# Seven products for two steps in layer A's pairs of heads, and the scores' second transposition put ahead of them

## The chip, the cores and the metric

The kernel runs on one core of a Trainium2 chip. The metric is the device time of one execution in microseconds (us), the median of several runs; lower is better.

## The reference

Two layers over x of 256 rows and 2048 columns, fp32, 32 heads of 128. What matters here, cut down:

```python
# layer A
h = rms_norm(x, a_norm)
q, k, v, g = split(h @ a_w_in, 4)             # 2048 -> 4 x 4096
o = chunked attention(q, k, v, rel_bias)      # chunks of 64, bias by distance
x = x + (o * silu(g)) @ a_w_out               # 4096 -> 2048
# shared keys and values, forget gates
k, v = split(rms_norm(x, kv_norm) @ kv_w, 2); logf = log_sigmoid(h_kv @ f_w + f_b)
# layer B
q, g = split(rms_norm(x, b_norm) @ b_w_in, 2)
o = causal attention(q, k, v) with decay from cumsum(logf)
x = x + (o * silu(g)) @ b_w_out
return rms_norm(x, final_norm)
```

## The kernel before

**Products.** Every fp32 weight and activation is split into a high and a low part (fp32r), and a product is three matmuls: high x high, low x high, high x low. Activations lie on the partitions transposed (`xTh`, `xTl`: normalised x of layer A), 256 rows are two tiles of 128. A *unit* is 512 output columns. In layer A each pair of heads g (0 to 15) has two units, `aqk{g}` (q and k) and `avg{g}` (v and gate). Their inner dimension of 2048 is done in 8 *steps* of two blocks of 128 (`KB`); a step is 2 blocks x 2 row tiles x 3 = 12 matmuls of 128x512 into `acc[0]`, `acc[1]` (PSUM).

**Feed.** SyncE's queue loads each step's weights (512 KB) into one of six `raw` buffers. ScalarE writes the high part (L247), VectorE the low part (L248); both go to one of `SPLIT = 4` buffers, so that a step's split can begin only when TensorE is through with the step four places before. `get()` hands a step to TensorE and keeps the splits three ahead (`DEPTH`).

**Quads.** In the output projections (`ao`, `bo`) some steps of two units go as a *quad*: four blocks of a 2x2 product (two row tiles, two k blocks) for two units by seven products in place of eight, as Winograd's form of Strassen's scheme has it. Two raw buffers `one` and `two` (the same step of the first and second unit) give four items: `one`; the differences `t` (L287, L288); half of `two`; and differences written back into `one` (L296, L297). Each is split like a step (L293 high, L294 low, the third with half the size). The left sides are the blocks of the activations and their sums (`sums`, made by `open`). Seven products of three matmuls are 21 instead of 24. Three go straight into `acc`; the others (p1, p5, p7, p6) stay in PSUM and are put together in `comb` at the end, which is then added to the units' results.

**Order.** Each engine runs its instructions in the order in which they stand, written down by a scheduling layer from the program's order. The attention of pair g runs as a generator (`side_a`) during pair g+1; the tables `QK_STEPS`, `PV_STEPS`, `OLD_A_STEPS` say after which step how many of its parts are issued. Its parts: `turn` of q and k (a VectorE transposition of 32x32 blocks and 16 small DMAs, into `turned`), splits (`wideh`/`widel`, `q1h`/`q1l`, `q0`), scores (`s1p`, `s0p` on TensorE), softmax (`sg`: scale and bias, maximum, exponentials, reciprocal, and the gate scaled by it), a second `turn` (`sgY`, 16 DMAs to `sgZ`), its split, the product with v (`op`), gating. When a unit ends, ScalarE evacuates `qk` from PSUM (L495), and `close_vg` makes v (`vh`, `vl`, `v1`) and the gate (`gs`) from `avg`'s accumulators. `feed.behind` ties an instruction to a place in ScalarE's order by a tiny write that reads a split's high part.

**Projections.** `xin` is the residual input of an output unit; it is loaded with four steps left, in one buffer (tag `R`) that several tiles share. At the end of a unit of `ao`, VectorE adds `comb` (L751) and the accumulators (L753) to it; its rows are transposed into `x1T`, the last unit's by TensorE (`x_to_T`, L169) inside the first steps of layer B, where `bqg0` already runs.

Of the kernel before, what the change touches and what calls it, by code (L numbers as in the profile page):

```python
# [16 lines left out]
P = 128  # L17
# [38 lines left out]

QK_STEPS = {0: 1, 6: 1, 7: 2}
PV_STEPS = {1: 1}
OLD_A_STEPS = {0: 1, 2: 99}
B1_STEPS = {3: 1, 5: 1, 6: 2}  # L60
# [15 lines left out]
def trunk(ctx, tc, x, x_t, gains, a_w_in, a_rel, a_w_out, kv_w, f_w, f_b, b_w_in, b_w_out, final_norm, out):  # L76
# [200 lines left out]
    class Quad:  # L277
# [4 lines left out]
        def split(self, i):  # L282

            one, two = self.raw
            t = self.all.t[:, 0]
            if not i:
                dve.tensor_sub(t[:, :, 0], two[:, :, 0], one[:, :, 0])  # L287
                dve.tensor_sub(t[:, :, 1], two[:, :, 1], two[:, :, 0])  # L288
            src = [one, t, two[:, :, 1:], one][i]
            n = src.shape[2]  # L290
            hi = stream.tile([P, IL, KB, HN], F32R, name=f"quad_hi{i}", tag="hi", bufs=SPLIT)
            lo = stream.tile([P, IL, KB, HN], F32R, name=f"quad_lo{i}", tag="lo", bufs=SPLIT)
            act.activation(hi[:, :, :n], src, AF.Copy)  # L293
            dve.tensor_sub(lo[:, :, :n], src, r32(hi[:, :, :n]))  # L294
            if not i:
                dve.tensor_sub(one[:, :, 0], two[:, :, 1], t[:, :, 0])  # L296
                dve.tensor_sub(one[:, :, 1], one[:, :, 1], one[:, :, 0])  # L297
            return hi, lo

        def step(self, lhs, first, second):  # L300
# [33 lines left out]
            if self.last:  # L334
                c = q.comb = q.t.rearrange("p r a j n -> p (r a j n)").rearrange("p (i n) -> p i n", n=UN)
                act.activation(c[:, 0], p1, AF.Copy)
                dve.tensor_add(c[:, 3], c[:, 0], p6)
                dve.tensor_add(c[:, 2], c[:, 3], p5)
                dve.tensor_add(c[:, 1], c[:, 3], p7)
                dve.tensor_add(c[:, 3], c[:, 1], p5)  # L340

    class Quads:


        def __init__(self, name, w):
            self.name, self.w, self.sums = name, w, []

# [10 lines left out]
        def open(self, lhs, n):  # L358


            self.t = big_tile([P, 2, IL, KB, HN], F32, f"{self.name}_quad")
            free = self.t[:, 1].rearrange("p a j n -> p (a j n)").rearrange("p (c i s) -> p c i s", c=2, s=P)
            xs, v = free[:, 0].rearrange("p (k t) s -> p k (t s)", t=NT), free[:, 1]
            for b in range(n):
                if b % 2 == 0:
                    two = big_tile([P, 2, 2, 4, P], F32R, f"{self.name}_sums{b}")
                self.sums.append(two[:, b % 2])
                hi, lo = two[:, b % 2, 0], two[:, b % 2, 1]
                k = b * KB
                dve.tensor_add(xs, r32(lhs.hi[k // BIG][:, k % BIG:k % BIG + KB]),  # L370
                               r32(lhs.lo[k // BIG][:, k % BIG:k % BIG + KB]))
                a11, a21, a12, a22 = (xs[:, j, t * P:(t + 1) * P] for j in range(KB) for t in range(NT))
                dve.tensor_add(v[:, 0], a21, a22)
                dve.tensor_sub(v[:, 2], a11, a21)
                dve.tensor_sub(v[:, 1], v[:, 0], a11)
                dve.tensor_sub(v[:, 3], a12, v[:, 1])
                act.activation(hi, v, AF.Copy)
                dve.tensor_sub(lo, v, r32(hi))
                yield

    def spec(name, w, nk, late=0, kept=0, g0=None):


        return dict(name=name, w=w, nk=nk, late=late, kept=kept, g0=g0)

    def whole(spec):
        return [(spec, b) for b in range(spec["nk"] // KB)]

    qkvg = []
    for g in range(NG):  # L390
        qkvg.append(spec(f"aqk{g}", a_w_in[2 * g], KD))
        qkvg.append(spec(f"avg{g}", a_w_in[2 * g + 1], KD))
    woven = [(qkvg[u], b) for u, b in WOVEN]
    todo = woven + [i for i in whole(qkvg[1]) if i not in woven]

    for sp_ in qkvg[2:]:
        todo += whole(sp_)
    ao = [spec(f"ao{u}", a_w_out[u], KI) for u in range(4)]
# [16 lines left out]
    class Unit:  # L415
# [3 lines left out]
        def __init__(self, lhs, sp_):  # L419
            self.lhs, self.nk, self.late = lhs, sp_["nk"], sp_["late"]  # L420
            self.acc = [ps_acc.tile([P, UN], F32, name=f"{sp_['name']}_acc{t}", tag="acc") for t in range(NT)]
            self.held, self.left, self.begun = [], self.nk // KB, set()

        def step(self, b):
            hi, lo = feed.get()
            hold = b >= self.nk // KB - self.late
            if hold:
# [14 lines left out]
    def rest(u):  # L442

        for b in range(u.nk // KB - u.left, u.nk // KB):
            u.step(b)
            yield u.acc
# [218 lines left out]
    def side_a(g, accs):  # L665
# [10 lines left out]
        qk = rows(UN, "qk")  # L676
        evac_scaled(accs["qk"], 0, UN, rsA, qk)
        yield
# [5 lines left out]

    def close_vg(accs):
        accs["v"] = v_split(accs["vg"], 0, rsA)
# [54 lines left out]
    def load_xin(src, u):  # L741
        xins[u] = att.tile([P, NT, UN], F32, name="xin", tag="R")
        sp.dma_start(out=xins[u], in_=src[:, :, u * UN:(u + 1) * UN])

    def ao_begun(u, left):
        if left == 4:
            load_xin(xf, u)

    def ao_closed(u, acc):
        cs, xin = slice(u * UN, (u + 1) * UN), xins.pop(u)  # L750
        dve.tensor_add(xin, xin, ao_quads.comb[:, u % 2 * NT:u % 2 * NT + NT])  # L751
        for t in range(NT):
# [164 lines left out]
    def bo_begun(u, left):  # L917
        if left == (4 if u else 1):
            load_xin(x1d, u)

    def bo_closed(u, acc):
        xin = xins.pop(u)
        if u > 1:
            dve.tensor_add(xin, xin, bo_quads.comb[:, u % 2 * NT:u % 2 * NT + NT])
        for t in range(NT):
# [53 lines left out]
```

## Time and profile before

| | us |
|---|---|
| median of 3 runs | 1765.71 (1765.02 to 1766.46) |
| the profiled execution | 1764.38 |
| its span | 1762.7 |
| TensorE busy | 1741.2 (99%) |
| VectorE busy | 1244.9 (71%) |
| ScalarE busy | 1108.3 (63%) |
| GpSimd busy | 516.8 (29%) |

The profiled execution is the one that all rows are from; 1.7 us of its time lie outside the span that the trace covers. PE is TensorE, DVE VectorE, ACT ScalarE, POOL GpSimd, SP SyncE. A row of a timeline is start, length, engine, line of the program, operation, out<-in, count, and in brackets the idle time before it with what ended it.

### The profile page before, as it was taken

How to read it: one execution, taken by the hardware profiler on the slowest of the kernel's cores; microseconds unless marked ns; L12 is line 12 of the kernel's file. 1: busy time of each engine (PE TensorE's matmuls, PEld its weight loads, DVE VectorE, ACT ScalarE, POOL GpSimd, SP SyncE). 2: the span in 40 equal slices, each digit the busy share in tenths (PEclk: the TensorE clock that was granted, in tenths of full speed). 3: DMA queues.
4: the chain of work that ended last, by engine and by line, in shares of the span. 5: the costliest groups of instructions: out<-in, count | busy, mean ns of one | idle time of the engine just before them, and what ended most of it. 6: DMA issues, size and time to landing. Idle time of an engine off the chain costs nothing.

```text
span 1762.7 us, 25633 instructions
## 1 busy us (share of the span) xinstructions
PE 1741.2 (99%) x8348; PEld 1531.0 (87%) x8348; DVE 1244.9 (71%) x1818; ACT 1108.3 (63%) x2102; POOL 516.8 (29%) x1071
## 2 busy tenths in 40 slices
PE   9999999999999999999999999999999999999997
PEld 7888888888888888887888888888888888888886
DVE  7666666666666686688877777777777777876687
ACT  6555555555555566556557777777777777765454
POOL 2333333333333333112104333333333333333000
PEclk9999999999999999999999999999999999999999
DMA  8777776767777677576767777776777777777664
GB/s 297 243 223 222 224 224 224 224 224 227 226 225 225 223 224 224 195 256 213 243 212 230 228 227 226 228 225 223 226 225 225 227 228 226 226 230 233 205 215 144
DMA packets 143653, 396.35 MB, mean 225 GB/s; under 512 B 31104, under 2 KB 38560, under 8 KB 143392
## 3 DMA queue, kind: packets, MB, share of 16 engines
q1 hardware_dynamic: 107472, 354.25, 63.1%
q0 software_dynamic: 32256, 37.29, 6.5%
q10 hardware_dynamic: 3792, 3.17, 0.6%
q8 instruction: 66, 1.08, 0.3%
q14 instruction: 67, 0.55, 0.1%
HBM read 351.05 MB, written 4.23 MB: 202 GB/s over the span
## 4 chain that ended last, share of the span: by engine, by line
PE 93%; DVE 3%; DMA 2%; issue 1%; ACT 1%; POOL 0%; ACTq 0%; SPq 0%; DVEq 0%; POOLq 0%
PE aqk_acc L184 19%; PE bkv_acc L184 19%; PE avg_acc L184 19%; PE bqg_acc L184 18%; PE bo_acc L184 6%; PE ao_acc L184 5%; PE op L574 1%; PE s0p L540 1%; DVE quad_lo L294 0%; DMA xinZ<-xinY 0%; PE op L517 0%; PE s1p L517 0%; PE s1p L516 0%; PE s1p L518 0%; PE op L518 0%
## 5 line engine op out<-in xcount | busy, mean ns | idle before, releaser
L489 POOL DMA_DIRECT2D sgZ<-sgY x512 | 251.0, 497 | 194.3 <-DVE sgY L486 90.6
L489 POOL DMA_DIRECT2D turned<-turned x448 | 219.9, 498 | 259.6 <-PE avg_acc L184 95.3
L243 DVE SCALAR_TENSOR_TENSOR bqg_lo<-bqg_raw,gain,bqg_hi 128x512 fp32r<-128x512 f32 x256 | 183.2, 753 | 84.3 <-ACT bqg_hi L242 84.2
L242 ACT ACTIVATE bqg_hi<-bqg_raw,gain 128x512 fp32r<-128x512 f32 x256 | 170.4, 714 | 106.7 <-PE bqg_acc L184 51.3
L248 DVE TENSOR_TENSOR avg_lo<-avg_raw,avg_hi 128x1024 fp32r<-128x1024 f32 x127 | 153.4, 1219 | 109.2 <-ACT avg_hi L247 108.0
L248 DVE TENSOR_TENSOR aqk_lo<-aqk_raw,aqk_hi 128x1024 fp32r<-128x1024 f32 x125 | 152.5, 1220 | 86.7 <-ACT aqk_hi L247 85.3
L247 ACT ACTIVATE avg_hi<-avg_raw 128x1024 fp32r<-128x1024 f32 x127 | 132.4, 1055 | 121.0 <-PE aqk_acc L184 68.5
L243 DVE SCALAR_TENSOR_TENSOR bkv_lo<-bkv_raw,gain,bkv_hi 128x512 fp32r<-128x512 f32 x256 | 181.2, 749 | 38.5 <-ACT bkv_hi L242 35.8
L184 PE MATMUL aqk_acc<-aqk_hi,xTh 128*128 128x512 f32 x512 | 191.4, 384 | 1.2 <-ACT aqk_hi L247 1.2
L184 PE MATMUL bqg_acc<-bqg_hi,x1Th 128*128 128x512 f32 x512 | 191.6, 384 | 0.0
L184 PE MATMUL avg_acc<-avg_hi,xTh 128*128 128x512 f32 x512 | 190.3, 382 | 0.0
L184 PE MATMUL aqk_acc<-aqk_lo,xTh 128*128 128x512 f32 x512 | 189.6, 381 | 0.0
L184 PE MATMUL aqk_acc<-aqk_hi,xTl 128*128 128x512 f32 x512 | 189.6, 381 | 0.0
L184 PE MATMUL bkv_acc<-bkv_hi,x1Th 128*128 128x512 f32 x512 | 189.2, 380 | 0.0
L184 PE MATMUL bqg_acc<-bqg_lo,x1Th 128*128 128x512 f32 x512 | 189.0, 379 | 0.0
L184 PE MATMUL bqg_acc<-bqg_hi,x1Tl 128*128 128x512 f32 x512 | 189.0, 379 | 0.0
L184 PE MATMUL bkv_acc<-bkv_lo,x1Th 128*128 128x512 f32 x512 | 189.0, 379 | 0.0
L184 PE MATMUL avg_acc<-avg_lo,xTh 128*128 128x512 f32 x512 | 189.0, 379 | 0.0
L184 PE MATMUL bkv_acc<-bkv_hi,x1Tl 128*128 128x512 f32 x512 | 189.0, 379 | 0.0
L184 PE MATMUL avg_acc<-avg_hi,xTl 128*128 128x512 f32 x512 | 189.0, 379 | 0.0
L247 ACT ACTIVATE aqk_hi<-aqk_raw 128x1024 fp32r<-128x1024 f32 x125 | 131.6, 1053 | 91.1 <-PE aqk_acc L184 43.5
L242 ACT ACTIVATE bkv_hi<-bkv_raw,gain 128x512 fp32r<-128x512 f32 x256 | 168.7, 712 | 22.9 <-PE bqg_acc L184 16.7
(297 smaller groups left out, 3563.8 us busy)
## 6 DMA issues: line engine op xcount, KB each, us to landing
bqg_raw<-in_b_w_in SPq DMA_DIRECT2D x128, 512.0 KB, 4.3
bkv_raw<-in_kv_w SPq DMA_DIRECT2D x128, 512.0 KB, 4.0
avg_raw<-in_a_w_in SPq DMA_DIRECT2D x127, 512.0 KB, 4.3
aqk_raw<-in_a_w_in SPq DMA_DIRECT2D x125, 512.0 KB, 4.2
ao_raw<-in_a_w_out SPq DMA_DIRECT2D x64, 512.0 KB, 4.4
bo_raw<-in_b_w_out SPq DMA_DIRECT2D x64, 512.0 KB, 4.2
sgZ<-sgY POOLq DMA_DIRECT2D x512, 40.0 KB, 4.1
turned<-turned POOLq DMA_DIRECT2D x448, 32.0 KB, 3.7
```

The costliest lines, as they stand in the source:

```text
L184: pe.matmul(acc[t], x[:, t * P:(t + 1) * P], w, start=t not in begun, stop=last and i == 2)
L242: act.activation(hi[:, :, j], raw[:, :, j], AF.Copy, scale=gk)
L243: dve.scalar_tensor_tensor(lo[:, :, j], raw[:, :, j], gk, r32(hi[:, :, j]), op0=OP.mult, op1=OP.subtract)
L247: act.activation(hi[:, :, j], raw[:, :, j], AF.Copy)
L248: dve.tensor_sub(lo[:, :, j], raw[:, :, j], r32(hi[:, :, j]))
L489: queues[j].dma_start(out=r32(z)[j * SQ:(j + 1) * SQ, i], in_=y[i * SQ:(i + 1) * SQ, j])
L540: pe.matmul(s0p[:, i], q0[:, i], qkT[:, HG + i, 0], start=True, stop=True)
L574: pe.matmul(op[:, i, P:], v1[:, i * DH:(i + 1) * DH], pT[:, i, NT], start=False, stop=i == HG - 1)
```

## The change

(1) In pairs 1 to 15 of layer A the last step of `aqk` and `avg` becomes a quad, done behind the third step of `aqk`. Both units' accumulators are taken at the pair's start. `comb` is scaled by the row norms on ScalarE; `qk` is then one VectorE operation per row tile (accumulator x norm + `comb`) instead of a ScalarE evacuation, and `close_vg` adds `comb` to `avg`'s accumulators first. (2) The scores stand behind the first step of the pair that follows instead of at the end of their pair; softmax and the second transposition are issued ahead of the quad's products. (3) `turned` is gone; its halves lie in the second half of the quads' scratch (`first1`) and of `sums`. (4) The sums of the activations are made once, in pair 0. (5) In every quad the first difference is tied by `behind`. (6) In the projections odd units' `xin` have a tile of their own, and `comb` is added to them with two steps left; layer B's first unit has the transpositions of the last `ao` unit one step later; two tables are shifted.

```diff
-QK_STEPS = {0: 1, 6: 1, 7: 2}
-PV_STEPS = {1: 1}
-OLD_A_STEPS = {0: 1, 2: 99}
+QUAD_STEP = 3
+SECOND_STEPS = {0: 1, 6: 1}
+FIRST_STEPS = {0: 2, 2: 1}
+OLD_A_STEPS = {1: 1, 3: 99}
...
@@ Quad.split
             if not i:
+                feed.behind(t[:, :, 0, :1], -1)
                 dve.tensor_sub(t[:, :, 0], two[:, :, 0], one[:, :, 0])
                 dve.tensor_sub(t[:, :, 1], two[:, :, 1], two[:, :, 0])
...
+    a_quads = Quads("a", None)
+    a_pairs = [Quad(a_quads, qkvg[2 * g:2 * g + 2], KD // KB - 1, True, True) for g in range(1, NG)]
+    for quad in a_pairs:
+        first, second = (whole(sp_) for sp_ in quad.specs)
+        todo += first[:QUAD_STEP] + [(None, quad)] + first[QUAD_STEP:] + second
...
-    sq = [big_tile([P, BIG, S], F32, name="sq0"), first[1].rearrange("p r a j n -> p (r a j) n")]
-    turned = big_tile([P, 2, NQ, 2 * HG * NT, SQ], F32, name="turned")
-    home = [turned[:, i] for i in range(2)]
+    a_quads.t, a_quads.comb = first[1], big_tile([P, 2 * NT, UN], F32, name="comb")
+    sums = big_tile([P, 2, 2, 4, P], F32R, name="sums")
+    home = [v.rearrange("p (i c u) -> p i c u", i=NQ, u=SQ) for v in
+            (first[1][:, 1].rearrange("p a j n -> p (a j n)"), sums[:, 1].rearrange("p a k s -> p (a k s)"))]
...
@@ side_a
-        evac_scaled(accs["qk"], 0, UN, rsA, qk)
+        if g:
+            for t in range(NT):
+                dve.scalar_tensor_tensor(qk[:, t], accs["qk"][t], rsA[:, t:t + 1], a_quads.comb[:, t],
+                                         op0=OP.mult, op1=OP.add)
+        else:
+            evac_scaled(accs["qk"], 0, UN, rsA, qk)
...
@@ close_vg
+        if g:
+            for t in range(NT):
+                whole_ = a_quads.comb[:, NT + t]
+                dve.tensor_add(whole_, accs["vg"][t], whole_)
+                accs["vg"][t] = whole_
...
         if g:
-            accs["qk"] = drive(unit(xT), prev, PV_STEPS)
-            vg = unit(xT)
+            first, second = (Unit(xT, next(order)) for _ in range(2))
+
+            def products():
+                a_pairs[g - 1].step(xT, first, second)
+                for t in range(NT):
+                    act.activation(a_quads.comb[:, t], a_quads.comb[:, t], AF.Copy, scale=rsA[:, t:t + 1])
+
+            accs["qk"] = drive(rest(first), prev, FIRST_STEPS, {QUAD_STEP - 1: products})
+            vg = rest(second)
...
-        accs["vg"] = drive(vg, prev, QK_STEPS, {}, old, OLD_A_STEPS)
-        close_vg(accs)
+        accs["vg"] = list(drive(vg, prev, SECOND_STEPS, {}, old, OLD_A_STEPS))
+        if not g:
+            a_quads.sum_up(xT, KD // KB - 1, sums[:, 0], a_quads.comb)
+        close_vg(accs, g)
...
-        xins[u] = att.tile([P, NT, UN], F32, name="xin", tag="R")
+        xins[u] = big_tile([P, NT, UN], F32, f"xin{u}") if u % 2 else att.tile([P, NT, UN], F32, name="xin", tag="R")
...
+        if left == 2 and u % 2:
+            add_combined(ao_quads, u)
...
-    project(oA, ao, ao_order, ao_begun, ao_closed, [(prev, [2, 6, 2, 1]), (ao_quads.open(oA, QUADS), [3, 1, 1, 2, 2])])
+    project(oA, ao, ao_order, ao_begun, ao_closed, [(prev, [1, 0, 2, 6, 2, 1]), (ao_quads.open(oA, QUADS), [3, 1, 1, 2, 2])])
...
-        accs["qg"] = drive(unit(x1T), prev if g else last[0], B1_STEPS if g else {1: 99}, {}, old, OLD_B_STEPS)
+        accs["qg"] = drive(unit(x1T), prev if g else last[0], B1_STEPS if g else {2: 99}, {}, old, OLD_B_STEPS)
```

In the orders below `_lo_` and `_hi_` are low and high parts, numbers after a name tell buffers apart, and lines are those of the program the rows are from: by the lines added above, L248, L486 and L547 of before are L249, L498 and L559 of the changed program, and L287, L288, L294, L296, L297 are L289, L290, L296, L298, L299.

VectorE of the program before, where a pair of layer A begins: the softmax of the pair before (`sg`, `nm`, `csc`) and its transposition `sgY` among plain low parts.

```order
L248 TENSOR_TENSOR aqk_lo_3843<-aqk_raw_3707,aqk_hi_3842 128x1024
L593 SCALAR_TENSOR_TENSOR vl<-avg_acc_3658,rstd_a,vh 128x256
L547 SCALAR_TENSOR_TENSOR sg<-s1p,tb 128x2x256
L547 SCALAR_TENSOR_TENSOR sg<-s0p,tb 128x2x128
L548 TENSOR_REDUCE nm<-sg 128x2 x2
L605 SCALAR_TENSOR_TENSOR gs<-gs,avg_acc_3658 128x256
L605 SCALAR_TENSOR_TENSOR gs<-gs,avg_acc_3659 128x256
L248 TENSOR_TENSOR aqk_lo_3895<-aqk_raw_3725,aqk_hi_3894 128x1024
L556 RECIPROCAL csc<-sm 128x4
L557 TENSOR_TENSOR csc<-csc,half_a 128x4
L248 TENSOR_TENSOR aqk_lo_3913<-aqk_raw_3757,aqk_hi_3912 128x1024
L486 STREAM_TRANSPOSE sgY<-sg 128x1280
```

One low part stands between the scores and the reciprocal, one between it and `sgY`. VectorE of the changed program, from the quad's second pair of differences (L298, L299) to the fourth plain low part of the pair:

```order
L298 TENSOR_TENSOR aqk_raw_3037<-avg_raw_3039,first_102 128x2x256
L560 TENSOR_REDUCE nm<-sg 128x2
L299 TENSOR_TENSOR aqk_raw_3037<-aqk_raw_3037 128x2x256
L559 SCALAR_TENSOR_TENSOR sg<-s0p,tb 128x2x128
L296 TENSOR_TENSOR quad_lo_3239<-first_102,quad_hi_3238 128x1024
L560 TENSOR_REDUCE nm<-sg 128x2
L296 TENSOR_TENSOR quad_lo_3255<-avg_raw_3039,quad_hi_3254 128x2x256
L568 RECIPROCAL csc<-sm 128x4
L569 TENSOR_TENSOR csc<-csc,half_a 128x4
L296 TENSOR_TENSOR quad_lo_3303<-aqk_raw_3037,quad_hi_3302 128x1024
L498 STREAM_TRANSPOSE sgY<-sg 128x1280
L249 TENSOR_TENSOR aqk_lo_3315<-aqk_raw_3080,aqk_hi_3314 128x1024
```

The whole softmax, `sgY` and the quad's differences and low parts now stand between two plain low parts (`aqk_lo`) of neighbouring steps. ScalarE of the changed program at the same place:

```order
L295 ACTIVATE quad_hi_3238<-first_102 128x1024
L562 ACTIVATE sg,sm<-sg,nm 128x256 x2
L295 ACTIVATE quad_hi_3254<-avg_raw_3039 128x2x256
L562 ACTIVATE sg,sm<-sg,nm 128x128 x2
L295 ACTIVATE quad_hi_3302<-aqk_raw_3037 128x1024
L573 ACTIVATE sg<-gs,csc 128x128 x4
L248 ACTIVATE aqk_hi_3314<-aqk_raw_3080 128x1024
```

Each high part of the quad (`quad_hi`) stands behind the exponentials (`sg,sm`) written ahead of it. TensorE of the changed program, from the quad's last product (`p`) into the fourth step of `aqk`:

```order
L528 MATMUL p_3301<-quad_hi_3302,sums 128x512
L529 MATMUL p_3301<-quad_lo_3303,sums 128x512
L530 MATMUL p_3301<-quad_hi_3302,sums 128x512
L185 MATMUL aqk_acc_3192<-aqk_hi_3314,xTh_105 128x512
L185 MATMUL aqk_acc_3193<-aqk_hi_3314,xTh_105 128x512
L185 MATMUL aqk_acc_3192<-aqk_lo_3315,xTh_105 128x512
L185 MATMUL aqk_acc_3192<-aqk_hi_3314,xTl_107 128x512
```

The fourth step, which stood directly behind the third, now stands behind the quad's 21 matmuls; the first matmul that reads its low part is the step's third.

More of the change, by code (lines that the diff above doesn't have):

```diff
@@ L366, in open @@
                     two = big_tile([P, 2, 2, 4, P], F32R, f"{self.name}_sums{b}")
[L367 to L378, printed above, removed]
-                yield
-    def spec(name, w, nk, late=0, kept=0, g0=None):
-        return dict(name=name, w=w, nk=nk, late=late, kept=kept, g0=g0)
+                self.sum_up(lhs, b, two[:, b % 2], free)
+                yield
+        def sum_up(self, lhs, b, dst, free):
+            self.sums[b] = dst
+            hi, lo = dst[:, 0], dst[:, 1]
+            xs, v = free[:, 0].rearrange("p (k s) -> p k s", s=S), free[:, 1].rearrange("p (i s) -> p i s", s=P)
+            k = b * KB
+            dve.tensor_add(xs, r32(lhs.hi[k // BIG][:, k % BIG:k % BIG + KB]),
+                           r32(lhs.lo[k // BIG][:, k % BIG:k % BIG + KB]))
+            a11, a21, a12, a22 = (xs[:, j, t * P:(t + 1) * P] for j in range(KB) for t in range(NT))
+            dve.tensor_add(v[:, 0], a21, a22)
+            dve.tensor_sub(v[:, 2], a11, a21)
+            dve.tensor_sub(v[:, 1], v[:, 0], a11)
+            dve.tensor_sub(v[:, 3], a12, v[:, 1])
+            act.activation(hi, v, AF.Copy)
+            dve.tensor_sub(lo, v, r32(hi))
@@ L386, in whole, with spec @@
+    def spec(name, w, nk, late=0, kept=0, g0=None, quads=0):
+        return dict(name=name, w=w, nk=nk, late=late, kept=kept, g0=g0, plain=nk // KB - quads)
     def whole(spec):
-        return [(spec, b) for b in range(spec["nk"] // KB)]
+        return [(spec, b) for b in range(spec["plain"])]
     qkvg = []
     for g in range(NG):
-        qkvg.append(spec(f"aqk{g}", a_w_in[2 * g], KD))
-        qkvg.append(spec(f"avg{g}", a_w_in[2 * g + 1], KD))
+        qkvg.append(spec(f"aqk{g}", a_w_in[2 * g], KD, quads=g > 0))
+        qkvg.append(spec(f"avg{g}", a_w_in[2 * g + 1], KD, quads=g > 0))
@@ L442, in rest @@
     def rest(u):
-        for b in range(u.nk // KB - u.left, u.nk // KB):
+        for b in range(u.done, u.plain):
             u.step(b)
@@ L919, in bo_begun @@
             load_xin(x1d, u)
+        if left == 2 and u == 3:
+            add_combined(bo_quads, u)
     def bo_closed(u, acc):
+        if u == 2:
+            add_combined(bo_quads, u)
         xin = xins.pop(u)
-        if u > 1:
-            dve.tensor_add(xin, xin, bo_quads.comb[:, u % 2 * NT:u % 2 * NT + NT])
         for t in range(NT):
```

23 lines of the change are left out of this document (13 added, 10 removed).

## The prediction

> **What bounds the kernel now.** I read the busy shares first, then the chain of work that ended last, then one pair of layer A in it, then every wait of TensorE.
>
> ```profile
> PE 1741.2 (99%) x8348; PEld 1531.0 (87%) x8348; DVE 1244.9 (71%) x1818; ACT 1108.3 (63%) x2102; POOL 516.8 (29%) x1071
> PE 93%; DVE 3%; DMA 2%; issue 1%; ACT 1%; POOL 0%; ACTq 0%; SPq 0%; DVEq 0%; POOLq 0%
> ```
>
> TensorE is busy for 99% of the span and carries 93% of the chain: where it never waits, only fewer matmuls help. The chain over one pair (start, length, count), then all engines over the same stretch:
>
> ```profile
> 404.15 20.72 PE aqk_acc L184 x96
> 424.88 7.77 PE avg_acc L184 x36
> 433.81 12.95 PE avg_acc L184 x60
> 447.93 20.72 PE aqk_acc L184 x96
> ```
> ```profile
> 404.15:447.93 43.78, 43.78 (x214) 38.70 (x213) 28.25 (x37) 25.85 (x47) 13.89 (x29) 1.00 0.72 225
> ```
>
> A pair takes 43.78 us. One matmul is 20.72/96 = 0.2158, a step of 12 is 2.59. The two gaps, for `op` (424.88+7.77 to 433.81) and for the scores `s1p`, `s0p` (446.76 to 447.93), are 1.17 each. TensorE (second column) never waits; VectorE has 28.25 us of work (fourth), ScalarE 25.85. What TensorE did wait for elsewhere:
>
> ```profile
> PE xT L169 <- DVE xin L753: 2.9, 2, 2.7
> PE op L516 <- ACT wideh L508: 2.6, 2, 2.2
> PE ao_acc L184 <- DVE ao_lo L248: 2.2, 1, 2.2
> PE bo_acc L517 <- DVE quad_lo L294: 0.9, 1, 0.9
> ```
>
> **The quads: what they take away.** Two plain last steps are 24 matmuls, a quad is 21: 3 x 0.2158 = 0.65 us less in each of 15 pairs, 9.7 us in all. This is certain work off the bound.
>
> **The quads: what they add, and where.** VectorE durations come from its busiest stretch in a pair of before; since short instructions overlap by about 0.1 us, the distance from one start to the next is what a queue of them costs:
>
> ```profile
> 447.59 0.69 DVE L547 SCALAR_TENSOR_TENSOR sg<-s1p,tb 128x512 f32<-128x512 f32 x1 [0.33 <-PE s1p L518]
> 448.20 0.41 DVE L547 SCALAR_TENSOR_TENSOR sg<-s0p,tb 128x256 f32<-128x256 f32 x1
> 448.53 1.00 DVE L548 TENSOR_REDUCE nm<-sg 128x2 f32<-128x512 f32 x2
> 449.45 0.74 DVE L605 SCALAR_TENSOR_TENSOR gs<-gs,avg_acc 128x256 f32<-128x256 f32 x2
> 450.11 1.22 DVE L248 TENSOR_TENSOR aqk_lo<-aqk_raw,aqk_hi 128x1024 fp32r<-128x1024 f32 x1
> 451.24 0.17 DVE L556 RECIPROCAL csc<-sm 128x4 f32<-128x4 f32 x1
> 451.45 0.16 DVE L557 TENSOR_TENSOR csc<-csc,half_a 128x4 f32<-128x4 f32 x1
> 453.25 1.51 DVE L486 STREAM_TRANSPOSE sgY<-sg 128x1280 f32<-128x1280 f32 x1
> 454.69 1.18 DVE L248 TENSOR_TENSOR aqk_lo<-aqk_raw,aqk_hi 128x1024 fp32r<-128x1024 f32 x1
> ```
> ```profile
> 802.96 0.69 DVE L297 TENSOR_TENSOR ao_raw<-ao_raw 128x512 f32<-128x512 f32 x1
> 803.56 1.22 DVE L294 TENSOR_TENSOR quad_lo<-ao_quad,quad_hi 128x1024 fp32r<-128x1024 f32 x1
> ```
> ```profile
> L509 DVE TENSOR_TENSOR widel<-turned,wideh 128x256 fp32r<-128x256 f32 x64 | 26.9, 421 | 19.4 <-ACT wideh L508 19.4
> L509 DVE TENSOR_TENSOR q1l<-turned,q1h 128x128 fp32r<-128x128 f32 x64 | 18.3, 285 | 0.0
> L593 DVE SCALAR_TENSOR_TENSOR vl<-avg_acc,rstd_a,vh 128x256 fp32r<-128x256 f32 x16 | 7.7, 479 | 0.1
> ```
>
> So a full low part costs 1.13, a half one or any 128x512 operation 0.60, the reduces 0.59 and 0.33, `sgY` 1.44, the score operations 0.61 and 0.33, a `gs` 0.33; `vl` about 0.40 and the four of `widel`/`q1l` 1.07 (busy less 0.08 each). Per pair VectorE gets 1.7 more low parts (1.9 us), 4 differences, 4 additions into `comb`, 2 in `close_vg`, 2 operations for `qk`: 12 x 0.60, so 28.25 becomes about 37 of a period of 43.13. It fits as a mean; the place decides. ScalarE gets some 2.3 us more (1.7 high parts, the copy of p1, four scalings, less the old evacuation of `qk`): 28, uncritical as a sum.
>
> All of it but the additions into `comb` and `qk` lands between low part a2 (third plain step) and a3 (fourth, behind the quad), together with `sgY`, which comes forward here. Let t = 0 be the first matmul of the pair. TensorE without a wait: a0 to 2.59, scores to 3.76, a1, a2 to 8.94, quad (21) to 13.47, then a3, whose third matmul needs a3's low part at **13.90**. The start is tied to TensorE as well: a2's high part needs the buffer that the step before last of `avg` gives back at -2.59. ScalarE's rows:
>
> ```profile
> 450.24 0.39 ACT L550 ACTIVATE sg<-sg,nm 128x128 f32<-128x128 f32 x1
> ...
> 451.01 1.04 ACT L247 ACTIVATE aqk_hi<-aqk_raw 128x1024 fp32r<-128x1024 f32 x1
> 451.96 1.26 ACT L561 ACTIVATE sg<-gs,csc 128x128 f32<-128x128 f32 x4
> 453.15 1.06 ACT L247 ACTIVATE aqk_hi<-aqk_raw 128x1024 fp32r<-128x1024 f32 x1
> ...
> 455.79 1.06 ACT L247 ACTIVATE aqk_hi<-aqk_raw 128x1024 fp32r<-128x1024 f32 x1 [1.58 <-PE aqk_acc L184]
> ```
>
> The last row starts 0.25 us behind the end of three steps counted from the first matmul (447.77 + 7.77 = 455.54). So a2's high part ends at -2.59 + 0.25 + 1.06 = -1.28, its low part starts at -1.26, and VectorE must do from there: four full low parts (a2, q0, q1, q3) 4.52, half of q2 0.60, `widel`/`q1l` 1.07, two additions 1.20, `vl` 0.40, two `gs` 0.66, three differences 1.80, scores 0.94, reduces 0.92, reciprocal and multiply 0.37, `sgY` 1.44, low a3 1.22: 15.14 us. That ends at 13.88: with no idle moment at all it is just in time. Two idle moments are forced. Laid in the order shown, the second reduce ends at about 9.20; the exponentials behind it take 0.77 (450.24 to 451.01) and end at 10.00, while VectorE is through with q2 at 9.72 and waits for its reciprocal until 10.12 (0.40). ScalarE takes q3's high part only behind these exponentials, to 11.05, and VectorE, done at 10.49, waits until 11.08 (0.59). Then q3's low part to 12.21, `sgY` to 13.65, a3's to 14.87. TensorE waits 0.97 us. A restart costs a further tenth:
>
> ```profile
> 804.84 0.48 PE L517 MATMUL p<-quad_lo,ao_sums 128*128 128x512 f32 x1 [0.29 <-DVE quad_lo L294]
> 805.15 0.38 PE L518 MATMUL p<-quad_hi,ao_sums 128*128 128x512 f32 x1
> ```
>
> (0.31 to the next start, not 0.216). So +1.07 - 0.65 = +0.42 per pair, x 15 = **+6.3 us**. It comes back in every pair, since the start is tied to TensorE's own steps. I hold the stall to 0.4 to 1.7: twenty prices, each good to some 0.03, and a wait more or less on the way.
>
> **What else moves.** Later deadlines in the pair hold: a4 is due 2.59 after a3, and a low part takes 1.13. `L290`, the second difference, is not tied and stands one step before the pair's start, where it waits for its load; four low parts queue behind it, and by the rows above it has some 1.5 us to spare (0; 0 to +0.7 a pair). The transposed scores, now issued some 4 us later against TensorE's steps, are needed by `op` one step later; the 16 transfers of `qk` land about 4 us ahead of use. `sums` is made once in the first pair, under VectorE's idle third (0; up to +1). The added tie is a ScalarE instruction of about 0.2.
>
> In pair 1 `op` waited 1.0 of the 2.6 above; behind one step more of cover I take -1.0 (-1.0 to 0). In the output projection of A the 2.2 us wait came from a difference waiting for its load ahead of low parts; the first difference is now tied, but `L290` takes that place in VectorE's order: 0 (-4 to +2). At the start of B:
>
> ```profile
> 876.45 6.37 DMA xin<-in_x
> ```
> ```profile
> ACT x1Th L150 <- DMA xinZ<-xinY: 3.1, 1, 3.1
> ```
>
> the last unit's `xin` was loaded only when its buffer came free, at 876.45, and the transpositions waited the 2.9 us shown. With a tile of its own it loads a unit earlier, and they stand a step later, so this wait goes. Next is the third unit's turned part, for which ScalarE already waited 3.1: -1.5 (-2.9 to 0). The same separation in B's output projection hides behind TensorE; 0 (-0.5 to 0.5).
>
> Sum: -9.7 + 16.0 - 1.0 - 1.5 = +3.8 on the profiled execution's 1764.38 (span 1762.7 and 1.7 around it): 1768.2. It lies 1.3 under the median 1765.71, so **1769.5 us**. What this kernel's measurements can tell is about 0.2%, 3.5 us; I stand at that line, on the slow side.
>
> **Rivals.** First, VectorE keeps up (faster). If the idle moments shrink, say because q3's high part gets ahead or short operations overlap more than by 0.1, the stall falls to 0.2: 15 x (0.2 - 0.65) - 2.5 = -9.2, **1756.5**. The quads pay once the stall is below 0.65, and by more than 0.2% once below 0.58. For it: 15.14 us of work in 15.16 of time. Against: three instructions in a row each wait for another engine.
>
> Second, the short stalls bring TensorE's clock down. Windows (the number behind the engines is the granted clock):
>
> ```profile
> 810.00:815.00 5.00, 3.81 (x12) 3.13 (x13) 5.00 (x5) 0.00 (x0) 2.36 (x6) 0.73 0.78 265
> 880.00:885.00 5.00, 2.86 (x14) 2.16 (x12) 2.06 (x3) 1.21 (x2) 1.90 (x4) 1.00 0.84 289
> 1545.00:1550.00 5.00, 2.83 (x16) 2.42 (x17) 2.76 (x6) 3.37 (x7) 2.68 (x7) 1.00 0.52 169
> ```
>
> After the 2.2 us wait of the projection, itself preceded by waits of 0.29 and 0.34, the clock was 0.73: matmuls at nearly half pace, some 1.7 us. Behind waits of 2.7 and 2.2 in the other two windows it stayed 1.00. If each quad's stall did the same, 15 x 1.7 = 25 more: **1795**. One place in three shows it, with a stall twice as long, so I give it little. The Trainium skill, "TensorE: Matmul & The Clock Gate", section "A second HAM failure mode: psum-queue depth-cycling", says that micro-idles between groups of matmuls can be frequent enough for the clock to oscillate. By that rule this rival would be the outcome; the steady 1.00 in two of the three windows does not bear it out.
>
> Third, a second wait joins (slower): `L290`'s load comes late, or `sgY`'s later transfers hold `op`. At +0.7 a pair that is 10.5 more: **1780**.
>
> **How the numbers follow.** The forecast, stall about 1.07 (0.8 to 1.4), 0.52: 1765.5 to 1774.5; a third of it lies within 0.2%. VectorE keeps up 0.24; clock 0.08; second wait 0.16. Faster by over 0.2%: 0.22; within: 0.18; slower: 0.60. The range leaves out the clock and the best of the first rival: 1755 to 1781.
>
> **What would show it.** Right: in a pair, TensorE's wait list names the plain low part of `aqk` with about 15 waits of 0.9 to 1.0, right behind the quad; VectorE without idle ahead of it but for the reciprocal and q3; a pair period near 44.2 in place of 43.78; clock 1.00; no `xT` wait of 2.7. A period of 43.13 to 43.3 means that VectorE kept up; a clock below 0.95 in layer A the second rival. I am wrong if one price, above all `sgY` or the gap at q3, is off by half a us.

## The result and the profile after

The changed kernel takes 1777.15 us (median of 6 runs, 1774.78 to 1779.84), the kernel before in the same comparison 1766.41 (1765.02 to 1767.22): ratio 1.0063, 95% interval 1.0052 to 1.0075. It is 10.7 us slower; 3.8 were forecast. The profiled execution took 1779.84 (span 1778.0), the slowest of the six, so the two traces, which the tables below compare, differ by 15.4 and not by 10.7.

The page after, the busy shares and the chain:

```profile
PE 1740.0 (98%) x8303; PEld 1516.0 (85%) x8303; DVE 1373.4 (77%) x2034; ACT 1136.2 (64%) x2176; POOL 520.7 (29%) x1071
PE 71%; DVE 13%; DMA 8%; issue 3%; ACT 3%; POOL 2%; SPq 0%; DVEq 0%; ACTq 0%; POOLq 0%
```

TensorE's share of the chain fell from 93% to 71%; VectorE now carries 13%, transfers 8%. TensorE has fewer matmuls and is waiting for the engines that feed it. What it waits for (total us, times, longest):

```profile
PE aqk_acc L185 <- DVE aqk_lo L249: 12.0, 16, 0.8
PE ao_acc L185 <- DVE ao_lo L249: 5.3, 3, 2.1
PE p L529 <- DVE quad_lo L296: 3.0, 2, 1.6
PE aqk_acc L529 <- DVE quad_lo L296: 2.5, 4, 0.8
PE bo_acc L529 <- DVE quad_lo L296: 1.8, 1, 1.8
```

Of the 16 waits of the first row 14 are the stall behind the quad, one in each of pairs 2 to 15; the other two lie in pair 0. In pair 1 TensorE's matmuls stand in another order, and it waits 0.25 and 0.28 there, for other parts. From the first matmul of each stage in the two timelines:

| stage | before | after | difference | forecast |
|---|---|---|---|---|
| pairs 1 to 15 of layer A | 659.3 | 670.0 | +10.7 | +5.3 |
| A's output projection | 167.2 | 177.7 | +10.5 | 0 |
| first pair of B | 50.6 | 47.2 | -3.3 | -1.5 |
| last pair of B | 46.7 | 43.8 | -2.9 | 0 |
| the rest | 838.9 | 839.4 | +0.5 | 0 |

Pair by pair in layer A: 8 of the last 14 pairs take 44.37 to 44.45, against 43.77 before; the others 44.5 to 46.0; pair 1 went from 46.51 to 44.42. So 14 x 0.60 = 8.4, 4.4 more in the irregular pairs, and 2.1 back in pair 1.

VectorE in a regular pair of the kernel after (first matmul of the pair at 95.37):

```profile
94.12 1.23 DVE L249 TENSOR_TENSOR aqk_lo<-aqk_raw,aqk_hi 128x1024 fp32r<-128x1024 f32 x1 [0.34 <-ACT aqk_hi L248]
...
105.63 0.18 DVE L568 RECIPROCAL csc<-sm 128x4 f32<-128x4 f32 x1 [0.35 <-ACT sg L562]
...
106.58 1.23 DVE L296 TENSOR_TENSOR quad_lo<-aqk_raw,quad_hi 128x1024 fp32r<-128x1024 f32 x1 [0.57 <-ACT quad_hi L295]
107.75 1.51 DVE L498 STREAM_TRANSPOSE sgY<-sg 128x1280 f32<-128x1280 f32 x1
109.18 3.45 DVE L249 TENSOR_TENSOR aqk_lo<-aqk_raw,aqk_hi 128x1024 fp32r<-128x1024 f32 x3
```

and TensorE there:

```profile
107.86 0.48 PE L529 MATMUL aqk_acc<-quad_lo,xTh 128*128 128x512 f32 x1
...
109.04 0.59 PE L185 MATMUL aqk_acc<-aqk_hi,xTh 128*128 128x512 f32 x2
110.42 0.48 PE L185 MATMUL aqk_acc<-aqk_lo,xTh 128*128 128x512 f32 x1 [0.78 <-DVE aqk_lo L249]
110.74 0.38 PE L185 MATMUL aqk_acc<-aqk_hi,xTl 128*128 128x512 f32 x1
```

The queue is as laid in the prediction: third low part 1.25 ahead of the pair's first matmul (forecast 1.26), the two forced idle moments 0.35 and 0.57 (0.40 and 0.59), the fourth low part from 13.81 (13.65). The third matmul of the fourth step is due two matmuls (0.216 each, from start to start) behind 109.04, at 109.47, and starts at 110.42: 0.95. The bracket's 0.78 is less, since it counts from the modelled end of the matmul before. The restart costs 0.10 (0.32 to the next start), and at 107.86 and 108.18 the quad's last low part cost 0.10 each: 1.25 in all, less 0.65, is the 0.60 that each regular pair lost.

### The profile page after: what moved, and what is told of

It is laid out like the page before. It is cut to its first block, busy times and chain, and to the rows that moved or that the text cites. A ratio compares the mean times of both kernels' runs of the same rounds, so it can differ in the third digit from the quotient of the medians.

```text
span 1778.0 us, 25837 instructions
## 1 busy us (share of the span) xinstructions
PE 1740.0 (98%) x8303; PEld 1516.0 (85%) x8303; DVE 1373.4 (77%) x2034; ACT 1136.2 (64%) x2176; POOL 520.7 (29%) x1071
## 4 chain that ended last, share of the span: by engine, by line
PE 71%; DVE 13%; DMA 8%; issue 3%; ACT 3%; POOL 2%; SPq 0%; DVEq 0%; ACTq 0%; POOLq 0%
PE bkv_acc L185 19%; PE bqg_acc L185 19%; PE aqk_acc L185 10%; PE bo_acc L185 7%; PE avg_acc L185 7%; PE ao_acc L185 4%; DVE quad_lo L296 3%; DMA avg_raw<-in_a_w_in 3%; DVE aqk_lo L249 2%; DMA sums<-first 2%; POOL sums L501 1%; DMA aqk_raw<-in_a_w_in 1%; ACT quad_hi L295 1%; DVE comb L708 1%; DVE nm L560 1%
## 5 line engine op out<-in xcount | busy, mean ns | idle before, releaser
L501 POOL DMA_DIRECT2D sums<-first x448 | 220.7, 499 | 226.2 <-PE bqg_acc L185 86.6
L243 ACT ACTIVATE bqg_hi<-bqg_raw,gain 128x512 fp32r<-128x512 f32 x256 | 170.8, 714 | 108.8 <-PE bqg_acc L185 51.4
L248 ACT ACTIVATE avg_hi<-avg_raw 128x1024 fp32r<-128x1024 f32 x112 | 118.0, 1054 | 116.1 <-issue 57.1
L185 PE MATMUL aqk_acc<-aqk_lo,xTh 128*128 128x512 f32 x452 | 167.8, 383 | 12.0 <-DVE aqk_lo L249 12.0
L249 DVE TENSOR_TENSOR avg_lo<-avg_raw,avg_hi 128x1024 fp32r<-128x1024 f32 x112 | 135.4, 1216 | 53.4 <-ACT avg_hi L248 53.4
L185 PE MATMUL avg_acc<-avg_hi,xTh 128*128 128x512 f32 x452 | 167.4, 382 | 0.0
L185 PE MATMUL aqk_acc<-aqk_hi,xTh 128*128 128x512 f32 x452 | 165.5, 383 | 1.9 <-ACT aqk_hi L248 1.9
L185 PE MATMUL avg_acc<-avg_hi,xTl 128*128 128x512 f32 x452 | 166.1, 379 | 0.0
L185 PE MATMUL aqk_acc<-aqk_hi,xTl 128*128 128x512 f32 x452 | 166.1, 379 | 0.0
L185 PE MATMUL avg_acc<-avg_lo,xTh 128*128 128x512 f32 x452 | 166.1, 379 | 0.0
L249 DVE TENSOR_TENSOR aqk_lo<-aqk_raw,aqk_hi 128x1024 fp32r<-128x1024 f32 x110 | 130.5, 1213 | 2.5 <-ACT aqk_hi L248 2.1
L248 ACT ACTIVATE aqk_hi<-aqk_raw 128x1024 fp32r<-128x1024 f32 x110 | 112.0, 1047 | 28.2 <-PE avg_acc L185 21.9
```

The source lines that it names most:

```text
L185: pe.matmul(acc[t], x[:, t * P:(t + 1) * P], w, start=t not in begun, stop=last and i == 2)
L243: act.activation(hi[:, :, j], raw[:, :, j], AF.Copy, scale=gk)
L248: act.activation(hi[:, :, j], raw[:, :, j], AF.Copy)
L249: dve.tensor_sub(lo[:, :, j], raw[:, :, j], r32(hi[:, :, j]))
L501: queues[j].dma_start(out=r32(z)[j * SQ:(j + 1) * SQ, i], in_=y[i * SQ:(i + 1) * SQ, j])
```

## The experiments

In this section "wait" is TensorE's, "pair" the time between the first matmuls of two pairs, and the edits are against the changed kernel unless said. What a kernel is compared with was timed again on the same chip (1764.2 to 1766.2).

**One difference twice, one difference left out.**

```diff
# e_more
                 dve.tensor_sub(one[:, :, 0], two[:, :, 1], t[:, :, 0])
+                if self.all is a_quads:
+                    dve.tensor_sub(one[:, :, 0], two[:, :, 1], t[:, :, 0])
# e_less
+                if self.all is not a_quads:
                     dve.tensor_sub(one[:, :, 1], one[:, :, 1], one[:, :, 0])
```

> The changed kernel with one of the quad's differences in layer A's pairs computed twice (the same value): 0.60 us more for VectorE between the third and the fourth low part, nothing else. If the stall is the end of VectorE's queue in that stretch, it comes 0.6 later in every pair: wait at the fourth step 0.78 to 1.4, pair 44.37 to 45.0. Rival, a fixed cost of a quad, or TensorE waiting for something else: pair stays at 44.4.

> The changed kernel with one difference (the write-back of the second half of one raw buffer) left out in layer A's quads, so their fourth factor is not the right one: 0.60 us less for VectorE in the stretch. If the stall is the end of VectorE's queue: wait 0.78 to about 0.2 and pair 44.37 to 43.8. Rival: pair stays at 44.4.

With 0.60 us more, the pair did not grow: 44.32, a single run, 1776.96. With 0.60 less it shrank to 43.98, a single run, 1771.55. Neither is the 0.6 expected. VectorE with one difference more (first matmul of the pair at 360.50; this pair takes 44.45):

```profile
371.07 0.17 DVE L570 RECIPROCAL csc<-sm 128x4 f32<-128x4 f32 x1
371.27 0.17 DVE L571 TENSOR_TENSOR csc<-csc,half_a 128x4 f32<-128x4 f32 x1
371.35 1.22 DVE L296 TENSOR_TENSOR quad_lo<-aqk_raw,quad_hi 128x1024 fp32r<-128x1024 f32 x1
372.96 1.51 DVE L500 STREAM_TRANSPOSE sgY<-sg 128x1280 f32<-128x1280 f32 x1 [0.38 <-ACT sg L575]
```

The scheduling layer had put the second reduce ahead of the low part q1, so the exponentials ran earlier: both idle moments are gone and one of 0.38 stands ahead of `sgY`. Work +0.60, idle 0.92 to 0.38: net +0.06. The fourth low part starts 13.89 after the first matmul in the pair shown, and 13.76 in the nine pairs that take 44.31 or 44.32, against 13.81 in the changed kernel: the dose came to nothing. With one difference less the idle moments are still 0.35 and 0.57, and in the regular pairs the fourth low part starts 0.60 earlier (13.21). But in that order the low part's first matmul is the fourth step's second, no longer its third, so it is due 0.22 earlier: 0.60 - 0.22 = 0.38 of the 0.39 measured. As a dose, neither kernel was clean.

The changed kernel itself holds a cleaner one, its irregular pairs, in which VectorE's queue is late from the start. The fourth low part starts at 13.81 in the regular pairs, at 14.52, 15.24 and 15.44 in pairs 5, 9 and 14; these take 44.37, 45.07, 45.80 and 46.00, later by as much. What sets the stall is the end of VectorE's queue, work and forced idle together; a fixed cost of a quad would have left all of these pairs at 44.37.

**The tie taken away.**

```diff
-                feed.behind(t[:, :, 0, :1], -1)
```

> The changed kernel without the tie of the quads' first difference. Both differences then stand in VectorE's order ahead of the pair's first low parts, so 0.60 us leaves the stretch between the third and the fourth low part. If VectorE's queue in that stretch sets the stall, the wait at the fourth step falls from 0.78 to about 0.2, the pair from 44.37 to about 43.8, 15 pairs give 9 us; in A's output projection both differences wait for a load ahead of low parts as they did before, one wait of about 2 in place of three: 178 us there becomes 168 to 172. Sum: 1777 - 9 - 7 = 1761. Rival, the stall is a fixed cost of a quad (its banks, its switch of operands): pairs stay at 44.3 to 44.4 and only the projection moves, 1768 to 1770.

Measured 1776.38 (ratio to before 1.0059, 1.0042 to 1.0076): no gain that can be told. The 15 pairs take 667.0 (3 less), the projection 174.3. Seven pairs take 44.0 to 44.2: they gain what the kernel with one difference less gained, since here too the low part's first matmul is the fourth step's second. In the others, 44.3 to 44.7 (and pair 14 with 46.5, of which below), the first difference has left the stretch but stands ahead of its beginning, waiting for its load:

```profile
178.79 0.69 DVE L288 TENSOR_TENSOR first<-avg_raw,aqk_raw 128x512 f32<-128x512 f32 x1 [3.58 <-DMA avg_raw<-in_a_w_in]
```

Three low parts, `oT` and `oAl` queue behind that wait, and `widel`, which else starts at the pair's first matmul, starts 0.59 behind it. My expectation had counted the stretch and not what is queued ahead of it.

**Both differences tied.**

```diff
                 feed.behind(t[:, :, 0, :1], -1)
+                feed.behind(t[:, :, 1, :1], -1)
```

> The changed kernel with the quads' second difference tied like the first. The order this gives has sgY behind the fourth low part (1.44 out of the stretch) and the second difference inside it (0.60 in); no difference stands ahead of plain low parts to wait for a load. VectorE's queue as the cause: stall at the fourth step zero to 0.2, pair 43.2 to 43.5, 15 pairs give 13 to 17 us, the pairs of 45 to 46 us go as well (2 to 3 us), the projection goes from 178 back to 167 or less (10 us): 1777 - 15 - 2 - 10 = 1750. Rival, the stall is a fixed cost of a quad: pairs stay at 44.3, 1764. Rival for the projection, the late attention of the last pair is at fault: it stays at 176 to 178, 1760.

Measured 1760.42: ratio to before 0.9965 (0.9952 to 0.9978), 17 us less than the changed kernel. VectorE behind the quad, in a pair from 441.01:

```profile
451.44 1.22 DVE L297 TENSOR_TENSOR quad_lo<-aqk_raw,quad_hi 128x1024 fp32r<-128x1024 f32 x1
452.57 0.17 DVE L569 RECIPROCAL csc<-sm 128x4 f32<-128x4 f32 x1
452.78 0.16 DVE L570 TENSOR_TENSOR csc<-csc,half_a 128x4 f32<-128x4 f32 x1
452.95 1.23 DVE L249 TENSOR_TENSOR aqk_lo<-aqk_raw,aqk_hi 128x1024 fp32r<-128x1024 f32 x1
454.29 1.51 DVE L499 STREAM_TRANSPOSE sgY<-sg 128x1280 f32<-128x1280 f32 x1
```

The reciprocal moved behind q3's low part, the fourth low part ahead of `sgY`. It starts 11.94 after the pair's first matmul, 1.9 earlier, and waits for nothing. Seven of the 15 pairs take 43.11 or 43.12, the 43.13 that 21 matmuls give without a stall; the 15 together 652.3, 17.7 less than in the changed kernel. Of the others, pair 1 takes 44.06, pair 14 44.82, and the rest lose 0.3 to 0.7, the pair shown 0.57 at `op`. TensorE's wait for `aqk`'s low part is down to one of 0.7 in pair 1. The projection stayed at 174.4, and there the expectation (167) was wrong.

**The second transposition a step later.**

```diff
-FIRST_STEPS = {0: 2, 2: 1}
+FIRST_STEPS = {0: 2, 3: 1}
```

> The changed kernel with the scores' second transposition issued one step later, behind the quad's products. sgY leaves the stretch ahead of the fourth low part. VectorE's queue as the cause: that wait is gone, pair 43.2 to 43.4, 15 pairs give 15 us; the projection's waits are untouched (178): 1777 - 15 = 1762. Rival, fixed cost of a quad: 44.3, no change, 1777. Second rival: the transposed scores come some 6 us later and the product with v waits for them, 1 to 3 us per pair in place of the stall: 1780 to 1800.

The second rival came true: 1782.85, ratio 1.0095 (1.0079 to 1.0112). The waits for the fourth low part are gone from pairs 2 to 15, and in their place stands

```profile
PE op L528 <- ACT wideh L520: 8.6, 12, 1.6
```

The order put `sgY` not one but four low parts later, among the additions into `comb`, so its 16 transfers landed late. One low part later, as with both differences tied, is late enough for the quad and early enough for `op`.

**The projections' edits alone**, on the kernel before: the tie, odd units' `xin` in tiles of their own, `comb` added earlier, the last transpositions one step later.

```diff
+                feed.behind(t[:, :, 0, :1], -1)
...
-        xins[u] = att.tile([P, NT, UN], F32, name="xin", tag="R")
+        xins[u] = big_tile([P, NT, UN], F32, f"xin{u}") if u % 2 else att.tile([P, NT, UN], F32, name="xin", tag="R")
...
+        if left == 2 and u % 2:
+            add_combined(ao_quads, u)
...
-B1_STEPS if g else {1: 99}
+B1_STEPS if g else {2: 99}
```

> The kernel before with the changes outside layer A's pairs alone: the first difference of the projections' quads tied, odd units' xin in tiles of their own, comb added two steps earlier, the last transpositions one step later. If the untied second difference, waiting for its load ahead of low parts, makes the projection of A slow, it goes from 167 to 174 to 178 here as well; the start of B gives 3.3: 1766.4 + 9 - 3.3 = 1772. Rival, the projection is slow because the last pair's attention now runs into it a step later: it stays at 167, and the start of B alone counts: 1763.

1761.14, ratio 0.9970 (0.9960 to 0.9981): 5 us faster. The projection took 169.8 (+2.6), where 174 to 178 was expected and 167 by the rival; the first pair of B 47.2 (-3.3), the last 44.8 (-1.9). So these edits alone are not what makes the projection slow in the changed kernel. Their price there:

```profile
802.19 1.25 DVE L487 STREAM_TRANSPOSE xinY<-xin 128x1024 f32<-128x1024 f32 x1 [6.95 <-DMA xinZ<-xinY]
```

With a tile of its own the second unit is done early, and its transposition stands in VectorE's queue waiting for the first unit's 16 transfers, with a quad's low parts behind it (before: 1.71; in the changed kernel 6.46).

**The pairs' quads alone**, with the projections as before the change (the tie for layer A's quads only, `xin` shared, `{1: 99}`).

> The changed kernel with the quads in layer A's pairs alone: in the projections no tie, no tiles of their own for xin, the last transpositions where they were. Pairs as in the changed kernel, 44.4 to 46. If the projection of A is slow because the last pair's attention runs into its first quads a step later, it stays at 174 to 178 and the start of B loses its 3.3: 1777 + 3 = 1780. Rival, the edits to the projections are at fault: projection 167 to 170, 1777 - 9 + 3 = 1771.

1777.64, ratio 1.0072 (1.0058 to 1.0085). Pairs as in the changed kernel (669.3), projection 172.0 and not the 174 to 178 expected, first pair of B 53.2, where the wait of `xT` is 3.7. The pairs' part alone costs the projection 4.8 and the other alone 2.6, in all 3.1 less than the +10.5 of both together. Most of these 3.1 us is the clock. In the trace it is granted at half for stretches of 3.41 us; the matmuls of such a stretch start 0.43 apart in place of 0.216, and 7 or 8 of them make 1.5 to 1.7 us. The projection holds one before the change (1.7), two in the changed kernel (3.2), two in a row with the projections' edits alone (11 matmuls, 2.4), and none with the pairs' quads alone. Less these amounts it takes 165.5, 174.5, 167.4 and 172.0: +9.0 together, +1.9 and +6.5 singly.

**The second unit's tile given back**, both differences tied, only the fourth unit's `xin` apart.

> The kernel with both differences tied (1760.4), but the second unit's xin of A's output projection in the shared buffer and with comb added at its end, as before the change; only the fourth unit keeps a tile of its own. If the separate tile of the second unit is what makes the turned rows of the first unit land late (waits of 1.3, 1.6 and 0.3 at the second set's first quad), those waits shrink to the 0.3 of before, the projection goes from 174 to 171: 1757. Rival, they land late because the last pair's attention and the quads' order moved: projection stays at 174, 1760.

1760.58, ratio 0.9975 (0.9964 to 0.9986): no change against 1760.42, and no 1757. VectorE's wait for the turned rows is nearly gone (0.85), but the old one stands again:

```profile
794.73 1.23 DVE L780 TENSOR_TENSOR xin<-xin,ao_quad 128x1024 f32<-128x1024 f32 x1 [4.42 <-DMA xin<-in_x]
```

TensorE still waits 1.95 and 1.18 at the second set's first quad, where 0.3 was expected, and the projection takes 176.7 in the profiled execution, the slowest of the seven. A tile of its own trades a wait for a load against a wait for transfers.

**The first quads of the projection two steps later**, once alone and once with both differences tied.

```diff
-    ao_order = ao_quads.order(ao[0], ao[1], 3, 13) + ao_quads.order(ao[2], ao[3], QUADS, 4)
+    ao_order = ao_quads.order(ao[0], ao[1], 3, 15) + ao_quads.order(ao[2], ao[3], QUADS, 4)
```

> The changed kernel with the first quads of A's output projection two steps later (15 plain steps ahead instead of 13). If the projection is slow because the last pair's gating, now a step later, stands among the first quad's VectorE work and so delays the release of its buffers and the next quads' loads, the waits of 2.1 and 1.0 at the second and third quad go, with the clock dip behind them: 178 to 172 or 173, total 1772. Rival, the loads of a quad's second buffer are late whatever stands there (the untied difference alone): waits stay, 1777.

> The kernel with both differences tied (1760.4) with the first quads two steps later. By the same reasoning the waits of 0.3 and 0.5 in the first set go and some of the 1.0 at the product with v; the second set's waits (1.3, 1.6, 0.3, 2.1, 0.8) stay: 1 to 2 us less, 1759. Rival, the set of three quads now runs into the end of the first two units: 1 to 3 us more, 1763.

Alone: 1772.20, ratio 1.0047 (1.0032 to 1.0063), as expected; the projection falls from 177.7 to 170.8. The waits of 2.1 and 1.0 in the first set are gone. The chain of the changed kernel shows what had made them:

```profile
757.31 0.68 DVE oT L590 x2
...
758.01 0.64 ACT oAh L594
...
758.67 0.69 DVE oAl L595
759.37 0.61 DVE quad_lo L296
...
759.99 3.23 DMA ao_raw<-in_a_w_out
...
763.25 0.03 DVE ao_quad L290
...
763.86 1.23 DVE ao_lo L249
765.09 0.04 issue
765.13 2.04 PE ao_acc L185 x4
```

The gating of the last pair (`oT`, `oAh`, `oAl`), a step later than before, stands inside the first quad. It holds back the low part that frees a raw buffer, the next load starts only then, and the next quad's second difference waits for it with three low parts behind.

With both differences tied: 1756.54, ratio 0.9952 (0.9939 to 0.9966); projection 172.9, pairs 652.1. This is the fastest version here, 7.7 us under the kernel before (1764.21 in that comparison). The pairs take 7.2 less than before the change, so the saving of the quads is real; the order in which the change put VectorE's work had spent it. Of the 7.7 in all, 5.0 are what the projections' edits gain when made alone.

## Why the prediction was right, and where its terms were off

The direction and the range (1755 to 1781) held, and the stall behind the quad, with its two forced idle moments, is where the prediction had laid it. That the total fell inside the range is in part luck: 1777.15 lies above the 1765.5 to 1774.5 that were given to this outcome alone, the output projection, put at 0, cost as much as all the pairs, and two gains in B, of which a quarter was foreseen, took 6.3 back. Point by point:

- **The stall in a pair** was sized at 1.07 and measured 1.25. The part missed is two tenths at the quad's last low part, which the prediction gave no price: it was to end at 12.21, its first matmul is due at 12.39, and in the trace it starts at 12.49. +0.42 became +0.60 a pair, 8.4 over pairs 2 to 15 in place of 5.9.
- **The third rival, a second wait**, came partly true beside the forecast. `L290` waits for its load in all 15 pairs, and where the load lands latest it reaches TensorE:

```profile
DVE first L290 <- DMA avg_raw<-in_a_w_in: 48.6, 15, 4.8
```

  I had given it 1.5 us to spare and a price of 0 to 0.7 a pair. The spare was 0.2 to 0.5: in the regular pairs it starts 5.6 to 5.9 ahead of the pair's first matmul, and from 5.3 on its delay reaches TensorE. Of the 4.4 us of the irregular pairs it explains 2.6 (pairs 4, 5, 6, 9, 11 and 15, in which its end shifts all that follows), which is 0.2 a pair; with the second difference tied it waits for nothing. The largest part of the rest, 1.6 in pair 14, has nothing to do with it: there the sums for the projection's quads, which `open` makes on VectorE, stand ahead of the pair's first low parts (first matmul at 630.53):

```profile
630.31 0.69 DVE L379 TENSOR_TENSOR ao_quad<-oAh,oAl 128x512 f32<-128x512 f32 x1
630.92 1.22 DVE L249 TENSOR_TENSOR aqk_lo<-aqk_raw,aqk_hi 128x1024 fp32r<-128x1024 f32 x1
632.05 0.42 DVE L521 TENSOR_TENSOR widel<-sums,wideh 128x256 fp32r<-128x256 f32 x1
```

  `widel` starts 1.52 behind the pair's first matmul, in a regular pair 0.11 ahead of it. Every kernel here with quads in the pairs has this, tied or not (44.8 to 46.5 in pair 14); the prediction's sum holds no term for it. The 0.2 of pair 12 I cannot place.
- **The output projection of A** is the term that failed: "0 (-4 to +2)", measured +10.5. I had asked only whether the old wait would go, not what the attention of the last pair, moved a step back in every pair, would run into at the end of the layer. The later quads gave 6.9 of it back, 1.7 of that by one stretch of half clock less.
- **The start of B**: -1.5 taken, -3.3 measured; the lower bound was -2.9. The turned part of the third unit, which I had put next in line, did not hold TensorE: no wait for `xT` is left.
- **The last pair of B**: not seen at all, -2.9. It is a side effect of the new order on VectorE, in a pair that the diff does not touch. Before (first matmul of the pair at 1539.56):

```profile
1520.60 0.69 DVE L378 TENSOR_TENSOR bo_sums<-bo_quad,bo_sums 128x512 fp32r<-128x512 f32 x1
1521.21 0.69 DVE L547 SCALAR_TENSOR_TENSOR sg<-s1p,cb 128x512 f32<-128x512 f32 x1
1528.63 1.50 DVE L486 STREAM_TRANSPOSE sgY<-sg 128x1280 f32<-128x1280 f32 x1
1530.69 4.91 POOL L489 DMA_DIRECT2D sgZ<-sgY  x10 [0.44 <-issue]
```

  and after (1557.35):

```profile
1532.94 3.40 DVE L244 SCALAR_TENSOR_TENSOR bkv_lo<-bkv_raw,gain,bkv_hi 128x512 fp32r<-128x512 f32 x5
1536.25 0.68 DVE L559 SCALAR_TENSOR_TENSOR sg<-s1p,cb 128x512 f32<-128x512 f32 x1
1543.41 1.51 DVE L498 STREAM_TRANSPOSE sgY<-sg 128x1280 f32<-128x1280 f32 x1
1545.47 4.43 POOL L501 DMA_DIRECT2D sgZ<-sgY  x9 [0.98 <-PE bkv_acc L185]
```

  Before, sums for the quads of `bo` stand between the scores and the softmax; after, all of them stand behind the pair's first matmul. `sgY` comes 13.9 ahead of that matmul in place of 10.9, its transfers start 2.06 behind it both times, and the wait of 2.2 for `op` is gone. With the projections' edits alone `sgY` comes 12.4 ahead and the wait is 0.31. The prediction had laid no queue in layer B's pairs.
- **Pair 1**: -0.6 forecast (the wait of `op` gone, 1.0, and +0.42 for the stall), -2.1 measured; the waits of `op` are 1.0 of it, and the stall of the other pairs is not there.
- **The second rival, the clock**, is refuted in the pairs and came up in the projection. Windows behind a pair's stall and behind two waits of 2.1 of the changed kernel:

```profile
110.00:115.00 5.00, 4.58 (x21) 4.05 (x22) 5.00 (x7) 3.66 (x5) 4.64 (x10) 1.00 0.79 228
765.00:770.00 5.00, 4.87 (x15) 3.98 (x16) 4.78 (x6) 0.51 (x1) 0.00 (x0) 0.66 0.75 226
835.00:840.00 5.00, 5.00 (x21) 4.19 (x20) 3.86 (x6) 1.74 (x3) 2.46 (x5) 0.81 0.77 268
```

  The 14 stalls of 0.95 left the clock at 1.00. Behind the two of 2.1 it fell to 0.66 and 0.81 in windows of 5 us, which cost 1.5 and 1.7. So the oscillation that the Trainium skill describes in "TensorE: Matmul & The Clock Gate", section "A second HAM failure mode: psum-queue depth-cycling", quoted as speaking for this rival, did not come from one short gap per pair here.

The errors add to +5.4 in the pairs, +10.5 in the projection, -4.8 in B and +0.5 elsewhere: 11.6 on top of 3.8 makes the 15.4 between the two profiled executions. The medians lie 10.7 apart, since the profiled execution after was 2.7 above its median and the one before 2.0 below.

What stays open: how the +9.0 of the projection that are not clock divide among its waits, since only the first set's were taken away, and why the clock fell in some windows with 1.6 to 1.9 us of idle and not in others (see the last section). A version with a clean dose of VectorE work, its order held fixed, was not made; the irregular pairs stand in for it.

## What to carry to other kernels

Where a saving on the bound engine adds work to one that feeds it, lay that engine's queue between two moments tied to the bound engine, instruction by instruction, and count idle moments forced by a third engine: here 15.1 us of work just fitted into 15.2, and 0.9 of forced idle decided. Then follow what the new order pushes past the stage's end, into the next stage and into pairs that the diff doesn't touch; that was as large as the term laid with care. An order that loses may need one instruction elsewhere: tying one more difference, which moved one low part ahead of one transposition and freed the queue ahead of the quad, turned 0.6% slower into 0.35% faster.

## What the hardware showed that I had not expected

A single wait of 1.6 us of TensorE, in the kernel with the later transposition, was enough for a clock of 0.71 in the next five us:

```profile
355.00:360.00 5.00, 4.42 (x17) 3.60 (x18) 3.85 (x7) 3.09 (x5) 2.86 (x6) 0.71 0.61 184
```

while the kernel before held 1.00 behind waits of 2.2 and 2.7, and 14 stalls of 0.95 did nothing. The length of the wait alone doesn't decide it; where it falls does. In the twelve traces the clock drops 13 times between the start and the end of the work, each time to half for 3.41 us (once for two times 3.41), and each drop begins a whole number of 3.41 us after the clock was first granted in full: the two of the changed kernel lie 68.27 us apart, 20 times 3.413, those of the kernel with the later transposition 477.87, 140 times. Cut into such windows, first the changed kernel at a drop, then the kernel before around its wait of 2.7:

```profile
761.77:765.19 3.42, 1.28 (x7) 0.80 (x5) 1.94 (x3) 2.33 (x4) 0.00 (x0) 1.00 0.75 246
765.19:768.60 3.41, 3.41 (x8) 2.73 (x9) 3.41 (x4) 0.00 (x0) 0.00 (x0) 0.50 0.77 208
```
```profile
880.55:883.97 3.42, 2.31 (x11) 1.69 (x9) 1.03 (x1) 0.66 (x2) 1.35 (x3) 1.00 0.95 336
883.97:887.38 3.41, 1.59 (x11) 1.38 (x12) 3.38 (x6) 1.45 (x4) 0.98 (x2) 1.00 0.59 153
```

TensorE (first number behind the comma) idles 2.1 of the 3.4 us ahead of the drop. The longer wait is split over two windows, 1.1 and 1.8 us idle, and the clock stays. All ten windows with over 2.1 us of idle are followed by a drop; the other three drops follow 1.6, 1.8 and 1.9, while windows with up to 1.9 went without, so the idle time of a window is not all that counts.
